# Respacing the mixers' chains of a hybrid decoder layer (mLSTM and HGRN2), with a second tile for mLSTM weights

## The chip, the cores and the metric

The kernel runs on one core of a Trainium2 chip. The metric is the device time of one execution in microseconds; the median of three runs of the kernel before is 1390.99 us (1390.58 to 1394.05). Engines are named as in the profile: PE is TensorE (matrix products), DVE is VectorE, ACT is ScalarE, POOL is GpSimd, SP issues DMAs.

## The reference: what is computed

One layer of a decoder on 1056 rows: a prompt of 1024 rows and 8 short sequences of 4 rows (the samples), width 1024. Cut to what matters here:

```python
h = rmsnorm(x);  p = h @ w_in + b_in            # 1024 -> 4104 columns
# mLSTM, 4 heads of 128, chunks of rows, state C (128x128), n, m
qk = silu(causal_conv(p_qk, width 4));  q, k = split(qk)
D  = where(causal, F_t - F_s + ig_s, -inf);  m_t = max(F + m, max(D))
s_qk = (q @ k.T) * exp(D - m_t)
num  = exp(a - m_t) * (q @ C) + s_qk @ v        # and the same with n for den
C    = decay * C + (w_last * k).T @ v
out_a = sigmoid(o) * headnorm(num / max(|den|, exp(-m_t)))
# HGRN2, 4 heads of 128, state S (128x128)
f = lb + (1 - lb) * sigmoid(f_raw);  b = cumsum(log f)
A = causal(sum_k q_t k_s exp(b_t - b_s));  o = (q * exp(b)) @ S + A @ v
S = exp(b_L) * S + (k * exp(b_L - b)).T @ v
out_b = headnorm(o) * silu(g)
x = x + concat(out_a, out_b) @ w_out
y = rmsnorm(x + (silu(h2 @ w_gate) * (h2 @ w_up)) @ w_down),  h2 = rmsnorm(x)
```

The outputs are the rows of the prompt and of the samples and all new states.

## The kernel before, in words

Activations lie transposed: 128 features on the partitions, rows along the free axis. The 1056 rows are three blocks of 288 (256 prompt rows and the 32 sample rows), 384 and 384. Large products are done in three passes of fp32r halves: `emit_k` (L120 to L144) issues, for each of 8 k-tiles of a *unit*, the products HI by whi, LO by whi and HI by wlo (L135 to L137). A unit is one tile of 128 output features for one block. One head and one block of the input projection are four units; the order of the units is head by head, within a head block by block, first all of mLSTM, then all of HGRN2, then the output projection and the feed-forward part. PSUM has three banks for units (tag mm), four for the mixers (tag mx) and one more (so).

**Chains.** What the mixers do with a head's block is a Python generator, `mix_a(h, b)` for mLSTM and `mix_b(h, b)` for HGRN2. The schedule is static: each engine works through its instructions in the order in which they are emitted. `hook()` is called after every second k-tile of a unit and after its evacuation, so four times a unit and 16 times a block (in head 0 of mLSTM a block has a fifth unit for the gates). Each hook gives every active chain whose countdown has run out one step, in the order in which the chains were started; `yield n` ends a step and asks for the next one n hooks later. So the numbers at the `yield`s decide between which large products a chain's small products stand on TensorE, and what stands ahead of what in the queues of DVE, ACT and POOL. A chain of mLSTM starts at the end of its block's third unit, one of HGRN2 at the end of its second. Counting hooks from the chain's start (t = 0), mLSTM heads 1 to 3 did this before the change:

- t = 0: W (weights of the causal part, L519, L521) and qw on DVE and ACT
- t = 2: pS = k q (L528), pK and pV, transposes of k and v (L532, L535)
- t = 3: vt and kt out of PSUM, W times pS (L542 to L546)
- t = 6: pU = kt vt (L551); t = 7: the state C (L559, L561)
- t = 9: pO = W vt + qw C (L572, L574)
- t = 11: squares and the head's norm (L578 to L582, `norm_cols` L495 to L500, its power on POOL)
- t = 13: hn, pO scaled (L585); t = 19: pH, hn transposed (L590); t = 20: out (L592)

The waits are the rows of `MAW`: one for each block of head 0 and the fourth for heads 1 to 3.

An HGRN2 chain builds its decayed products by levels of doubling length (`prod`, `take`, `step`):

- t = 2, 6, 10: products of levels 0 and 1, 2 and 4, 8 and 16 (L777), each followed a hook later by `take` (L784) and one hook apart by two `step`s (L796, L798, L804 on DVE; ACT copies the other halves, L801, L802)
- t = 14: the cross products of levels 32 and 64 (L855, L860), which read what step 32 (t = 12) made
- t = 15: into AT (L865, L866), step 64; t = 16: pV, pK (L874, L877); t = 17: vt, kt
- t = 19: pU (L891); t = 20: state (L901); t = 22: pO (L911, L913)
- t = 23: squares and norm; t = 25: hn scaled (L923); t = 31: pH (L928); t = 32: out (L930)

Evacuations of a unit are emitted just before the hook at its end: for HGRN2 the forget gate at hook 3 of a block (two sigmoids on ACT, L743 and L744, and L745, L746 on DVE), q at hook 7, v at hook 11, the output gate at hook 15. In mLSTM q and k with their convolution on DVE stand at hooks 3 and 7, v at 11 and the output gate (L471 on ACT, L472 on DVE) at 15. Beside the chains run the samples' chains (`sample_a`, `sample_b`) in mLSTM's and HGRN2's last heads, the splitting of the coming weights (`split`, L96 on ACT and L97 on POOL), and once, ahead of (3, 1), the lower-bound constants (`lb_consts`, L259 to L268). The tile kt had one buffer, and hn was another use of the same tag; W had one buffer.

Of the kernel before, what the change touches and what calls it, by code (L numbers as in the profile page):

```python
# [9 lines left out]
F32 = mybir.dt.float32  # L10
# [13 lines left out]
NB = 3  # L24
H = 4
# [15 lines left out]
def hybrid_step(ctx: ExitStack, tc: tile.TileContext, i, o):  # L41
# [6 lines left out]
    mp = p1.enter_context(tc.tile_pool(name="mixp", bufs=1))  # L48
# [3 lines left out]
    def bank(tag="mx"):  # L52
        return psum.tile([128, 512], F32, tag=tag, name=tag, bufs={"mm": 3, "mx": 4, "so": 1}[tag])
# [136 lines left out]

    def ntile(tag="nt"):
        if tag in ("raw", "W"):
            return mp.tile([128, 387], F32, tag=tag, name=tag, bufs=2 if tag == "raw" else 1)
        if tag == "na":
            return cn.tile([128, QN], F32, tag=tag, name=tag, bufs=1)
        return cn.tile([128, 384], F32, tag=tag, name=tag, bufs=2)
# [43 lines left out]
    def tl(tag, n=384, bufs=2, dt=F32, p=128):  # L240
        return mp.tile([p, n], dt, tag=tag, name=tag, bufs=bufs)
# [250 lines left out]
    def norm_cols(s, sqs, nch, d2=None, p=128):  # L492
# [14 lines left out]

    def mix_a(h, b):
        w = MAW[b if h == 0 else 3]
# [3 lines left out]
        while ("gc", b) not in done or ("cv", "k") not in done:  # L513
            yield 1
        ng, wi = S["ng", h, b], S["wi", h, b]
        W = mp.tile([128, 387], F32, tag="W", name="W", bufs=1)
        for c in range(ncb):
            s = slice(c * 128, c * 128 + 128)
            nc.vector.scalar_tensor_tensor(W[:, s], ng[:, s], cols[:, c0 + c, 0, h:h + 1], maskneg,  # L519
                                           op0=OP.add, op1=OP.add)  # L520
        nc.scalar.activation(W[:, :npr], W[:, :npr], AF.Exp)  # L521
        qw = tl("qw")
# [14 lines left out]
        if (h, b) == (0, 0):  # L537
            nc.gpsimd.memset(ktm, 0.0)
        kt = tl("kt", 384, 1)
# [5 lines left out]
                                cols[:, c0:c0 + ncb, 2, h:h + 1].to_broadcast([128, ncb, 128]), op=OP.mult)  # L545
        nc.vector.scalar_tensor_tensor(W[:, :npr], pS[:, :npr], QS, W[:, :npr], op0=OP.mult, op1=OP.mult)  # L546
        yield w[2]
# [22 lines left out]
        for c in range(ncb):  # L570
            s = slice(c * 128, c * 128 + 128)
            nc.tensor.matmul(pO[:, c, 0:129], W[:, s], vt[:, c, 0:129], start=True, stop=cin[c] is None)  # L572
            if cin[c] is not None:
                nc.tensor.matmul(pO[:, c, 0:129], qw[:, s], cin[c], start=False, stop=True)  # L574
        yield w[5]
        sm = mp.tile([128, 3, 4], F32, tag="sm", name="sm", bufs=2)
        hn = tl("kt", 384, 1)
        nc.scalar.activation(sm[:, 1, :ncb, None], pO[:, :ncb, 128:129], AF.Square)  # L578
        for c in range(ncb):
            nc.scalar.activation(hn[:, c * 128:c * 128 + 128], pO[:, c, 0:128], AF.Square, accum_out=sm[:, 0, c:c + 1])  # L580
# [121 lines left out]
    def sample_a():  # L702
# [12 lines left out]
        for h in range(H):  # L715
            nc.tensor.matmul(pS[32 * h:32 * h + 32, 0:32], kS[:, h, :], qS[:, h, :], start=True, stop=True,
                             tile_position=(0, 32 * h))
        W = tl("sW", 32, 1)
        nc.vector.scalar_tensor_tensor(W, ngS, scol[:, 0:1], mneg4, op0=OP.add, op1=OP.add)
# [29 lines left out]
    def mix_b(h, b):  # L749
# [2 lines left out]
        AT, AD = ATs[atn[0] % 2], ADs[atn[0] % 2]  # L752
        atn[0] += 1
        samp = b == 0
        gx = tl("wib", 388, 2)
        qp = tl("qw")

# [32 lines left out]
        def step(lv, src, dst):  # L790

            nn = n if samp and lv <= 2 else npr
            G, go = gst
            nb = nn // (2 * lv)
            gv = G[:, go:go + nn // lv].rearrange("p (n two) -> p n two", two=2)
            nc.vector.tensor_tensor(odd(dst[0][:, :nn], lv), odd(src[0][:, :nn], lv), gv[:, :, 0:1].to_broadcast([128, nb, lv]),  # L796
                                    op=OP.mult)
            nc.vector.tensor_tensor(even(dst[1][:, :nn], lv), even(src[1][:, :nn], lv), gv[:, :, 1:2].to_broadcast([128, nb, lv]),  # L798
                                    op=OP.mult)
            if dst is not src:  # L800
                nc.scalar.activation(even(dst[0][:, :nn], lv), even(src[0][:, :nn], lv), AF.Copy)  # L801
                nc.scalar.activation(odd(dst[1][:, :nn], lv), odd(src[1][:, :nn], lv), AF.Copy)  # L802
            go2 = 0 if lv == 1 else go + nn // lv
            nc.vector.tensor_tensor(gx[:, go2:go2 + nb, None], gv[:, :, 0:1], gv[:, :, 1:2], op=OP.mult)  # L804
            gst[:] = gx, go2
# [59 lines left out]
            nc.scalar.activation(AT[s0:s0 + 32, :ncb, s0 + 32:s0 + 64], pc[s0:s0 + 32], AF.Copy)  # L865
        nc.scalar.activation(AT[0:64, :ncb, 64:128], ps[0:64, 128:128 + 64 * ncb].rearrange("p (c t) -> p c t", t=64), AF.Copy)  # L866
        step(64, B, B)
        yield 1
        go, qp, k = gst[1], qB, kB
        v = S["vb", h, b]  # L870
        pK, pV = bank(), bank()
# [7 lines left out]
        kt = tl("kt", 384, 1)  # L879
# [3 lines left out]
        if samp:  # L883
            nc.gpsimd.tensor_copy(ss_["sv"][:, h, :], v[:, 256:288])
            nc.gpsimd.tensor_copy(ss_["so"][:, h, :], S["g", h, b][:, 256:288])
        yield 2
        pU = bank()
        C = mp.tile([128, 3, 130], F32, tag="C", name="C", bufs=2)
        for c in range(ncb):
# [14 lines left out]
        Sst[h] = prev  # L904
        if b == 2:
            nc.sync.dma_start(o["Sp"][h], prev)
        yield 2
        pO = bank()
        for c in range(ncb):
            s = slice(c * 128, c * 128 + 128)  # L910
# [2 lines left out]
                nc.tensor.matmul(pO[:, s], qp[:, s], cin[c], start=False, stop=True)  # L913
        yield 1
        sm = mp.tile([128, 3, 4], F32, tag="sm", name="sm", bufs=2)
        hn = tl("kt", 384, 1)
        for c in range(ncb):
            nc.scalar.activation(hn[:, c * 128:c * 128 + 128], pO[:, c * 128:c * 128 + 128], AF.Square,
                                 accum_out=sm[:, 0, c:c + 1])
# [1 line left out]
        yield 2  # L921
        for c in range(ncb):
            nc.vector.tensor_scalar_mul(hn[:, c * 128:c * 128 + 128], pO[:, c * 128:c * 128 + 128], sm[:, 2, c:c + 1])  # L923
        yield 6
        pH = bank()
        for c in range(ncb):
            s = slice(c * 128, c * 128 + 128)
# [38 lines left out]
    for h in range(H):  # L966
        ts = [wtile(wa[17 + 4 * h + j]) for j in range(4)]
        for b in range(NB):
            evs = [f_evac(h, b), act_evac("qb", "cq", AF.Sigmoid, V_BIN + 16 + h, h, b, silu=True),
                   act_evac("vb", "v", AF.Identity, V_BIN + 24 + h, h, b),  # L970
                   act_evac("g", "go", AF.Sigmoid, V_BIN + 28 + h, h, b, 2, silu=True)]
            posts = [None, spawn((lambda h, b: lambda: mix_b(h, b))(h, b), "b", h, b), None, None]
            in_group(ts, b, evs, posts)
# [35 lines left out]
    def out_evac(m, q):  # L1009
        def ev(ps):  # L1010
            x = xq(q)
            nc.vector.tensor_tensor(x[:, m, :], x[:, m, :], ps[:, :QN], op=OP.add)
            dst = ntile(("raw", "raw", "W", "na")[q]) if m == 0 else ntile()
            nc.scalar.activation(dst[:, :QN], x[:, m, :], AF.Square)
            if m == 0:
                naccs[q] = dst
            else:
                nc.vector.tensor_tensor(naccs[q][:, :QN], naccs[q][:, :QN], dst[:, :QN], op=OP.add)
            if m in (4, KT - 1):
                s = slice(0, 5) if m == 4 else slice(5, KT)  # L1020
                nc.sync.dma_start(d_x[:, s, q * QN:(q + 1) * QN], x[:, s, :])
            if m == KT - 1:
                start(norm2(q), ("n2", q))
        return ev
# [22 lines left out]
    def gate_evac(f, q):  # L1047
        def ev(ps):
            if sgn[0] < 2 * NPLAIN - 2:
                t = sgt[f, q] = tl(SGT[sgn[0] % 3])  # L1050
                sgn[0] += 1
            else:
                t = sgt[f, q] = ntile()
            nc.scalar.activation(t[:, :QN], ps[:, :QN], AF.Silu)  # L1054
        return ev
# [913 lines left out]
```

## Time and profile before

| | |
|---|---|
| median of the runs | 1390.99 us |
| the profiled execution | 1389.23 us |
| its span | 1387.4 us |
| PE busy | 1333.1 us (96%) |
| DVE busy | 867.8 us (63%) |
| ACT busy | 558.2 us (40%) |
| POOL busy | 594.3 us (43%) |
| mixers: mLSTM heads 1 to 3 | about 128 to 305 us |
| mixers: HGRN2 | about 305 to 575 us |

Busy times are sums over one profiled execution. Products on PE are pipelined, so a busy PE only says that some product was under way; where PE waited is seen in the list of waits and in the distances between the starts of products.

### The profile page before, as it was taken

The page shows a single profiled execution, that of the slowest core. Times are in us where ns is not written, and L with a number is a line of the kernel's source. Part 1 is how long each engine was busy: PE and PEld are TensorE (multiplying, and loading weights), DVE is VectorE, ACT ScalarE, POOL GpSimd, SP SyncE. Part 2 cuts the span into 40 slices and gives each one's busy share as a digit, 9 for nine tenths or more (in the row PEclk, how much of TensorE's full clock was granted, in tenths as well). Part 3 has the DMA queues.
Part 4 walks back from the last instruction along what each step waited for, and adds up shares of the span by engine and source line. Part 5 has one row for each costly group of instructions (what it writes and reads, how often), then busy time and mean ns, then how long its engine had stood idle before and what let it go on. Part 6 is the DMA issues. An engine that isn't in the chain of part 4 may idle for free. (4 is left out here: it accounts for less than half of the span.)

```text
span 1387.4 us, 29406 instructions
## 1 busy us (share of the span) xinstructions
PE 1333.1 (96%) x11600; PEld 1301.1 (94%) x11600; DVE 867.8 (63%) x2060; ACT 558.2 (40%) x1315; POOL 594.3 (43%) x566
## 2 busy tenths in 40 slices
PE   7878999999999999999999999999999999999996
PEld 6878999899999998899998999999999999999995
DVE  7876667664545456644675667666665346777775
ACT  6554434233444344422435445544544341222232
POOL 5323212231222223212537666666656683544435
PEclk9999999999999999999999999999999999999998
DMA  6012222230101113554455657567654278878743
GB/s 227 23 33 63 69 63 74 82 115 17 49 32 35 46 49 116 150 161 125 159 188 194 214 207 259 204 218 253 215 211 167 78 268 317 306 270 293 286 153 125
DMA packets 109937, 212.12 MB, mean 153 GB/s; under 512 B 11088, under 2 KB 63848, under 8 KB 109288
## 3 DMA queue, kind: packets, MB, share of 16 engines
q1 hardware_dynamic: 109368, 209.98, 43.8%
q8 instruction: 91, 1.49, 0.5%
q14 instruction: 46, 0.38, 0.1%
q10 hardware_dynamic: 432, 0.27, 0.1%
HBM read 143.76 MB, written 66.45 MB: 152 GB/s over the span
## 5 line engine op out<-in xcount | busy, mean ns | idle before, releaser
L135 PE MATMUL mm<-HI,whi 128*128 128x384 f32 (+2 forms) x1160 | 378.6, 326 | 5.0 <-ACT gA L304 2.9
L137 PE MATMUL mm<-HI,wlo 128*128 128x384 f32 (+2 forms) x1160 | 362.7, 313 | 1.3 <-POOL wlo L97 1.3
L136 PE MATMUL mm<-LO,whi 128*128 128x384 f32 (+2 forms) x1160 | 362.7, 313 | 0.4 <-POOL LO L225 0.2
L135 PEld LDWEIGHTS mm<-HI,whi 128*128 128x128 f32 x1160 | 221.0, 191 | 10.2 <-ACT gA L304 3.2
L136 PEld LDWEIGHTS mm<-LO,whi 128*128 128x128 f32 x1160 | 221.1, 191 | 1.6 <-POOL LO L225 0.7
L137 PEld LDWEIGHTS mm<-HI,wlo 128*128 128x128 f32 x1160 | 220.7, 190 | 1.8 <-POOL wlo L97 1.8
L97 POOL TENSOR_TENSOR wlo<-raw,whi 128x512 fp32r<-128x512 f32 x90 | 118.6, 1328 | 217.5 <-ACT whi L96 172.6
L1199 POOL TENSOR_TENSOR wlo<-S,whi 128x512 fp32r<-128x512 f32 x78 | 110.6, 1424 | 87.5 <-ACT whi L1198 84.6
L1270 PE MATMUL mx<-T,whi 128*128 128x264 f32 x640 | 118.2, 284 | 0.0
L1323 POOL TENSOR_TENSOR LO<-rg,HI 128x528 fp32r<-128x528 f32 x52 | 71.2, 1379 | 65.7 <-ACT HI L1322 65.7
L1270 PEld LDWEIGHTS mx<-T,whi 128*128 128x128 f32 x640 | 99.0, 188 | 0.0
L1270 PE MATMUL mx<-HI,whi 128*128 128x264 f32 x320 | 91.1, 285 | 0.0
L1270 PE MATMUL mx<-HI,wlo 128*128 128x264 f32 x320 | 90.9, 284 | 0.0
L1270 PE MATMUL mx<-T,wlo 128*128 128x264 f32 x320 | 90.9, 284 | 0.0
L1270 PE MATMUL mx<-LO,whi 128*128 128x264 f32 x320 | 90.7, 283 | 0.0
L1411 DVE TENSOR_TENSOR fh<-fr,fh 128x512 fp32r<-128x512 f32 x80 | 67.1, 839 | 31.8 <-ACT fh L1406 31.5
L1497 DVE TENSOR_TENSOR X<-X,mx 128x264 f32<-128x264 f32 x160 | 65.6, 425 | 27.4 <-PE mx L1493 26.8
L1198 ACT ACTIVATE whi<-S 128x512 fp32r<-128x512 f32 x80 | 50.3, 630 | 68.2 <-DVE S L1187 68.1
L1322 ACT ACTIVATE HI<-rg 128x528 fp32r<-128x528 f32 x52 | 32.3, 642 | 105.9 <-PE mx L1493 32.5
L1270 PE MATMUL mm<-HI,whi 128*128 128x264 f32 x240 | 68.3, 284 | 1.2 <-ACT nt L1054 1.2
L1270 PE MATMUL mm<-HI,wlo 128*128 128x264 f32 x240 | 68.2, 284 | 0.0
L1270 PE MATMUL mm<-LO,whi 128*128 128x264 f32 x240 | 67.9, 283 | 0.0
(545 smaller groups left out, 3412.4 us busy)
## 6 DMA issues: line engine op xcount, KB each, us to landing
d_wf<-fh SPq DMA_DIRECT2D x60, 512.0 KB
rg<-d_ff SPq DMA_DIRECT2D x42, 528.0 KB
raw<-in_wA SPq DMA_DIRECT2D x31, 512.0 KB
whi<-d_wf SPq DMA_DIRECT2D x29, 512.0 KB
wlo<-d_wf SPq DMA_DIRECT2D x28, 512.0 KB
raw<-in_wgu SPq DMA_DIRECT2D x24, 512.0 KB
d_ff<-sg SPq DMA_DIRECT2D x40, 264.0 KB
rg<-in_wgu SPq DMA_DIRECT2D x20, 512.0 KB
```

Of the source, the lines that this page charges most:

```text
L97: (nc.gpsimd if pool else nc.vector).tensor_tensor(lo[:, s], raw[:, s], hi[:, s].bitcast(F32), op=OP.subtract)
L135: nc.tensor.matmul(ps[:, :n], wh, rh[:, k, :], start=(k == 0), stop=False)
L136: nc.tensor.matmul(ps[:, :n], wh, rl[:, k, :], start=False, stop=False)
L137: nc.tensor.matmul(ps[:, :n], wl, rh[:, k, :], start=False, stop=(k == nk - 1))
L1198: nc.scalar.activation(hi[:, s], t, AF.Copy)
L1199: (nc.vector if dve else nc.gpsimd).tensor_tensor(lo[:, s], t, hi[:, s].bitcast(F32), op=OP.subtract)
L1270: nc.tensor.matmul(ps[:, :QN], a[:, w], b_[:, kk, c], start=new and kk == 0 and x == 0, stop=kk == 3 and x == 2, skip_group_check=True)
L1322: nc.scalar.activation(h, src, AF.Copy)
L1323: (nc.vector if dve else nc.gpsimd).tensor_tensor(lw, src, h.bitcast(F32), op=OP.subtract)
L1411: nc.vector.tensor_tensor(lw, src, h.bitcast(F32), op=OP.subtract)
L1497: nc.vector.tensor_tensor(y, y, ps[:, :QN], op=OP.add)
```

## The change

Three edits. The row of waits for mLSTM heads 1 to 3 puts pO at t = 18 instead of 9, the squares at 19, hn at 21, pH at 22 and the output at 23. In HGRN2, for all blocks but the last one of the last head, pV and pK move to t = 18 (from 16), kt and vt to 19, pU to 22 (from 19), the state to 23, pO to 26 (from 22), squares to 27, hn to 29, pH to 30 (from 31) and the output to 31. And W gets a second buffer, hn a tile of its own.

```diff
@@ ntile
-            return mp.tile([128, 387], F32, tag=tag, name=tag, bufs=2 if tag == "raw" else 1)
+            return mp.tile([128, 387], F32, tag=tag, name=tag, bufs=2)
@@ MAW
-        (2, 1, 3, 1, 2, 2, 2, 6, 1))
+        (2, 1, 3, 1, 11, 1, 2, 1, 1))
@@ mix_a
-        W = mp.tile([128, 387], F32, tag="W", name="W", bufs=1)
+        W = mp.tile([128, 387], F32, tag="W", name="W", bufs=2)
...
-        hn = tl("kt", 384, 1)
+        hn = tl("hn", 384, 1)
@@ mix_b
+        w = (1, 2, 2, 6) if (h, b) == (H - 1, NB - 1) else (3, 3, 3, 1)
...
         step(64, B, B)
-        yield 1
+        yield w[0]
...
-        yield 2
+        yield w[1]
         pU = bank()
...
-        yield 2
+        yield w[2]
         pO = bank()
...
-        hn = tl("kt", 384, 1)
+        hn = tl("hn", 384, 1)
...
             nc.vector.tensor_scalar_mul(hn[:, c * 128:c * 128 + 128], pO[:, c * 128:c * 128 + 128], sm[:, 2, c:c + 1])
-        yield 6
+        yield w[3]
         pH = bank()
```

## The prediction

> **What bounds the kernel now.** I read the page first, then the busy time of the two mixer stretches, then TensorE's own waits there, and last the order in time around single places.
>
> ```profile
> span 1387.4 us, 29406 instructions
> ...
> PE 1333.1 (96%) x11600; PEld 1301.1 (94%) x11600; DVE 867.8 (63%) x2060; ACT 558.2 (40%) x1315; POOL 594.3 (43%) x566
> ```
>
> ```profile
> 109.10:115.90 6.80, 6.15 (x28) 6.05 (x29) 3.93 (x21) 4.13 (x16) 4.63 (x8) 0.50 0.42 135
> 128.00:305.00 177.00, 175.41 (x1230) 171.38 (x1229) 116.18 (x334) 66.91 (x183) 48.09 (x87) 1.00 0.26 79
> 305.00:620.00 315.00, 307.96 (x3729) 290.96 (x3729) 173.94 (x606) 120.76 (x367) 76.23 (x88) 1.00 0.23 70
> ```
>
> The columns are the stretch, its length, then busy time of PE, PEld, DVE, ACT and POOL, the granted clock, the DMA share and GB/s. From 128 to 305 us (mLSTM) TensorE is idle for 177.00 - 175.41 = 1.6 us, from 305 to 620 us (HGRN2 and the start of the output projection) for 7.0 us. Everything the mixers' chains put on TensorE stands between the large products of one stream without slack, so a microsecond that TensorE waits is a microsecond at the end, and one that it saves is gained. TensorE's waits of the two stretches:
>
> ```profile
> PE mx L574 <- DVE C L559: 1.6, 1, 1.6
> ```
>
> ```profile
> PE mx L860 <- DVE wib L804: 4.0, 5, 2.0
> PE mx L877 <- DVE kB L798: 1.0, 1, 1.0
> ```
>
> The chains are written so that their small products hardly ever find an input missing. The question is what the new spacing does to that.
>
> **The places, counted in hooks.** A block is 16 hooks, so step t of one block falls on step t - 16 of the next. For mLSTM heads 1 to 3 the products stood at t = 2, 6, 9, 19: four places in 16 hooks. Now they stand at 2, 6, 18, 22: two places, since 18 is 2 and 22 is 6 of the next block. The HGRN2 products stood at 2, 6, 10, 14, 16, 19, 22, 31, with only 22 falling on 6: seven places. Now they stand at 2, 6, 10, 14, 18, 22, 26, 30: four. That is 9 x 2 + 11 x 3 = 51 places fewer (the last HGRN2 block and head 0 of mLSTM keep their spacing). The instructions themselves, their sizes and the DMAs stay; the state stores move by no hook, and only the last mLSTM block's two small stores go three hooks later, past nothing that TensorE needs.
>
> **What a place is worth.** The trace has a pair of groups each alone and both in one place, in the same stream of 384 columns, whose products follow each other every 0.17 us:
>
> ```profile
> 410.38 0.34 PE L137 MATMUL mm<-HI,wlo 128*128 128x384 f32 x1
> 410.55 0.38 PE L928 MATMUL mx<-ident,kt 128*128 128x128 f32 x2
> 410.69 0.42 PE L135 MATMUL mm<-HI,whi 128*128 128x384 f32 x1
> 410.95 0.33 PE L136 MATMUL mm<-LO,whi 128*128 128x384 f32 x1
> ```
>
> ```profile
> 544.72 0.34 PE L137 MATMUL mm<-HI,wlo 128*128 128x384 f32 x1
> 544.99 0.42 PE L674 MATMUL so<-st,qz 128*32 128x128 f32 x8
> ...
> 545.63 0.34 PE L136 MATMUL mm<-LO,whi 128*128 128x384 f32 x1
> ```
>
> ```profile
> 540.03 0.34 PE L137 MATMUL mm<-HI,wlo 128*128 128x384 f32 x1
> 540.20 0.38 PE L928 MATMUL mx<-ident,kt 128*128 128x128 f32 x2
> 540.51 0.43 PE L674 MATMUL so<-st,qz 128*32 128x128 f32 x8
> ...
> 541.15 0.34 PE L136 MATMUL mm<-LO,whi 128*128 128x384 f32 x1
> ```
>
> From the last large product before to the second one after, less the two steps of 0.17 us that would be there anyway: L928 alone costs 410.95 - 410.38 - 0.34 = 0.23, L674 alone 545.63 - 544.72 - 0.34 = 0.57, both together 541.15 - 540.03 - 0.34 = 0.78. Sharing saves about 0.02 us at most, and by the clock of the trace (0.01 us) no more can be read. A return to the stream does show a longer first step (410.69 to 410.95 is 0.26 and not 0.17, so 0.09 us), but it is made up by the group's first product, which starts without a gap. I take 0.013 us, so 51 x 0.013 = 0.7 us gained; the bounds are nothing and 51 x 0.09 = 4.6 us. The Trainium skill, TensorE: Matmul & The Clock Gate, section "Step-by-step: what each phase is for", holds that a product alone cannot hide its drain while products in a stream do. By that rule each place pays about one drain of 128 cycles, an estimate of 0.05 us, and the change would gain an estimated 2.7 us; the pair above does not bear it out.
>
> **What the new spacing makes TensorE wait for: HGRN2.** pH (L928, t = 30) reads hn, which DVE scales at t = 29 (L923). Before, six hooks lay between; now it is one. t = 30 falls on 14 of the next block, and t = 29 on 13, so in DVE's order L923 comes behind that block's step 32 (t = 12: L796, L798, L804), which itself stands behind the evacuation of the next forget gate. Step 32 is today ready just as TensorE arrives at t = 14, or later:
>
> ```profile
> 403.62 0.60 DVE L923 TENSOR_SCALAR kt<-mx,sm 128x128 f32<-128x128 f32 x2
> ...
> 426.26 0.18 DVE L804 TENSOR_TENSOR wib<-wib 128x24 f32<-128x24 f32 x1
> 426.35 0.86 DVE L923 TENSOR_SCALAR kt<-mx,sm 128x128 f32<-128x128 f32 x3
> ...
> 430.19 0.38 PE L855 MATMUL mx<-qw,ck 128*32 128x32 f32 x12
> ...
> 430.55 0.16 DVE L804 TENSOR_TENSOR wib<-wib 128x6 f32<-128x6 f32 x1
> 430.79 0.53 PE L860 MATMUL mx<-qB,kB 128*32 128x64 f32 x12 [0.21 <-DVE wib L804]
> ```
>
> ```profile
> 408.71 0.16 DVE L804 TENSOR_TENSOR wib<-wib 128x6 f32<-128x6 f32 x1
> 408.72 0.38 PE L855 MATMUL mx<-qw,ck 128*32 128x32 f32 x12
> ...
> 450.54 0.32 PE L855 MATMUL mx<-qw,ck 128*32 128x32 f32 x8
> ...
> 450.73 0.15 DVE L804 TENSOR_TENSOR wib<-wib 128x4 f32<-128x4 f32 x1
> ```
>
> Three scalings behind L804 end 426.35 + 0.86 - 426.44 = 0.77 us after it, two (a 256-row block) 0.51; TensorE follows 430.79 - 430.71 = 0.08 later. pH now stands at the head of this place, so its wait counts from where L855 starts today:
> - 288-column stream (third block of a head): 430.71 + 0.77 + 0.08 - 430.19 = 1.37, of which 0.21 is waited today: 1.16 more, three times.
> - first block of a head (three scalings of the block before): 450.88 + 0.85 - 450.54 = 1.19, three times.
> - second block (two scalings): 408.87 + 0.59 - 408.72 = 0.74, three times.
> - the last head's second and third block already wait longest there (the 2.0 and most of the 4.0 us above). Behind the same late step 32 come two and three scalings: 0.59 and 0.85.
>
> That is 3.5 + 3.6 + 2.2 + 1.4 = 10.7 us. Behind pH on TensorE wait the cross products L855 and L860 and the whole stream; ACT's copies into AT and DVE's step 64 wait for those. No later wait absorbs it. The other three places of a block get easier, not harder: pO stands ahead of L777 at t = 10, and pK and pV have three hooks after step 64 where they had one, so the 1.0 us at L877 goes.
>
> **mLSTM.** hn is scaled at t = 21 and transposed at 22, which is t = 6 of the next block. Ahead of it in DVE's order is the evacuation of the output gate (L472), at the end of a unit two hooks earlier. Where TensorE arrives today at t = 6 (L551):
>
> ```profile
> 173.33 1.30 POOL L97 TENSOR_TENSOR wlo<-raw,whi 128x512 fp32r<-128x512 f32 x1
> 173.38 1.47 DVE L472 TENSOR_SCALAR go<-go 128x384 f32<-128x384 f32 x1 [0.75 <-ACT go L471]
> ...
> 174.06 0.50 PE L551 MATMUL mx<-vt,kt 128*128 128x129 f32 x3
> ...
> 208.62 0.36 DVE L472 TENSOR_SCALAR go<-go 128x384 f32<-128x384 f32 x1 [0.66 <-ACT go L471]
> ...
> 229.26 1.48 DVE L472 TENSOR_SCALAR go<-go 128x384 f32<-128x384 f32 x1 [0.93 <-ACT go L471]
> ...
> 229.77 0.50 PE L551 MATMUL mx<-vt,kt 128*128 128x129 f32 x3
> ...
> 246.88 0.61 PE L551 MATMUL mx<-vt,kt 128*128 128x129 f32 x4
> ...
> 249.00 1.46 DVE L268 TENSOR_SCALAR omlb<-lb 128x4 f32<-128x4 f32 x1
> ```
>
> Most of these places fit (the L472 of 208.62 ends at 208.98, and 0.85 later is before L551's usual time). Three do not. At 174.06: 174.85 + 0.85 - 174.06 = 1.64. At 229.77: 230.74 + 0.85 - 229.77 = 1.82. At 246.88 the sample chain's set-up and the lower-bound constants (up to L268) come between the two hooks: 250.46 + 0.85 - 246.88 = 4.43, and in return the 1.6 us that L574 waits a little later goes, as its product moves away. All three rows are long because POOL's L97 runs beside them (L472 is 0.36 when it does not); without it they are 1.1, 1.1 and 1.3 us shorter. I take half of that off, 1.8. A fourth is the first HGRN2 block's t = 10, shared with the last mLSTM transposes:
>
> ```profile
> 318.82 0.16 DVE L804 TENSOR_TENSOR wib<-wib 128x16 f32<-128x16 f32 x1
> 319.04 0.32 PE L777 MATMUL mx<-qw,ck 128*32 128x16 f32 x16 [0.91 <-DVE wib L804]
> ```
>
> The place begins at 319.04 - 0.91 - 0.32 = 317.81; pH would wait to 318.98 + 0.85 = 319.83, 2.0 us against the 0.91 of today: 1.1 more. Second tiles of W and a tile hn of their own only take waits off DVE and ACT; TensorE waits for neither today, so I cost them at nothing, and they are what makes the overlap of two blocks possible at all (without them kt and W of the next block would be held to t = 22).
>
> **Sum.** 10.7 + 1.64 + 1.82 + 4.43 + 1.1 - 1.8 = 17.9 lost, 1.6 + 1.0 + 0.7 = 3.3 gained: 14.6 us more. The profiled execution took 1389.23 us, 1.8 under the median of the runs (1390.99); 1389.2 + 14.6 = 1403.8 there, and 1405.5 against the median.
>
> **The rivals.**
> - *Places have a price of their own* (faster). If each place cost the 0.09 us of the longer first step, 4.6 us would be gained, with the 2.6 of the two waits 7.2: about 1384. For it speaks the row at 410.69; against it the shared place at 540, and that the new waits would have to be absent as well; with them it is 1391 + 14.6 - 3.9 = 1402.
> - *No change.* DVE gets so far ahead, with less of its work standing before the gate evacuations, that pH waits a third of the sum: 1391 + 17.9/3 - 3.3 = 1394, within the bound. Against it: L745 and L746 wait for the end of a TensorE unit, so no slack on DVE moves step 32.
> - *A smaller loss.* POOL's op misses all three rows and the last head's two places cost nothing: 14.6 - 1.8 - 1.4 = 11.4, and with half of the first-block waits gone 9.6: about 1400.
> - *The clock falls.* Today a wait of 4.42 us is followed by half the clock, the 0.50 of the stretch 109.10:115.90:
>
> ```profile
> 109.47 0.26 PE L346 MATMUL mx<-ident,gB 4*128 4x4 f32 x1 [4.42 <-ACT gB L334]
> ```
>
>   The new wait at 246.88 is as long. Half the clock over 6.8 us costs up to 3.4 us: 1409. The Trainium skill, TensorE: Matmul & The Clock Gate, section "Why this matters for your kernels", asks for no gap over about 3 us between bursts for this reason; the row agrees.
> - That the places do not coincide as said I exclude: the shared one of today (t = 22 on 6) stands in the trace where the count of hooks puts it.
>
> **How the numbers follow.** Forecast 0.50, clock 0.18, smaller loss 0.14, no change 0.07, faster 0.11. Faster by over 0.3% (4.2 us, about what a measurement tells from no change) 0.11, within it 0.07, slower 0.82. The forecast's own range is 1399 to 1411. To leave no more than 2 in 10 out, the range goes from 1394 (no change's upper half and the smaller loss are in) to 1412 (above it only a lowered clock at more than one place).
>
> **What would show it.** In the changed kernel's waits of TensorE, L928 (HGRN2 pH) should stand with DVE's scaling as releaser, some 11 times and about 1 us each, and L590 (mLSTM pH) with three or four times 1 to 4 us; L574 and L877 should be gone; the idle time of the two stretches should rise from 8.6 to over 20 us while PE's busy time stays within 1 us. It is wrong if TensorE's busy time falls by several us (places have a price), or if pH finds hn ready.

## The result

| | before | after |
|---|---|---|
| median of the runs, same session | 1391.83 us (1390.58 to 1394.05, 4 runs) | 1404.72 us (1401.22 to 1410.72, 4 runs) |
| the profiled execution | 1389.23 us | 1404.2 us |
| its span | 1387.4 us | 1402.2 us |

The changed kernel is slower: the ratio is 1.0102, with a 95% interval of 1.008 to 1.0124. Forecast were 1405.5 us and a chance of 0.82 for slower.

The page of the changed kernel, its span and the busy times:

```profile
span 1402.2 us, 29380 instructions
...
PE 1339.3 (96%) x11600; PEld 1304.7 (93%) x11600; DVE 868.8 (62%) x2060; ACT 560.0 (40%) x1315; POOL 593.2 (42%) x566
```

The same two mixer stretches after, and two short ones in them (columns as before: stretch, length, busy time of PE, PEld, DVE, ACT and POOL, granted clock, DMA share, GB/s):

```profile
128.00:305.00 177.00, 172.78 (x1188) 167.52 (x1187) 112.51 (x323) 65.67 (x174) 47.78 (x85) 0.99 0.25 76
305.00:620.00 315.00, 302.62 (x3655) 284.31 (x3654) 171.85 (x597) 119.71 (x367) 71.19 (x86) 0.99 0.22 66
253.30:256.70 3.40, 3.40 (x13) 3.40 (x12) 2.03 (x7) 0.00 (x0) 0.32 (x2) 0.51 0.66 220
581.00:584.40 3.40, 3.40 (x24) 3.23 (x19) 3.16 (x9) 1.84 (x5) 0.91 (x1) 0.50 0.78 225
```

TensorE is idle for 4.2 us of the first stretch (1.6 before) and 12.4 us of the second (7.0 before). In the two short stretches it is busy throughout, but at half the clock: between 253.3 and 256.7 us the large products start every 0.32 us instead of every 0.173, so 3.4 us of half clock cost 3.4 x (1 - 0.173/0.32) = 1.6 us. TensorE's waits after, in the mLSTM stretch and then in the HGRN2 stretch (line, releaser, us in all, times, longest):

```profile
PE mx L590 <- DVE hn L585: 4.2, 3, 3.3
```

```profile
PE mx L929 <- DVE hn L924: 9.6, 10, 2.0
PE mx L929 <- ACT whi L96: 1.6, 1, 1.6
PE mx L696 <- DVE sjunk L693: 0.6, 1, 0.6
PE so L674 <- DMA st<-in_S: 0.5, 1, 0.5
PE mx L861 <- DVE wib L805: 0.2, 1, 0.2
```

From mix_b on, the lines of the changed kernel stand one further down: L929 is HGRN2's pH (L928 before), L924 its scaling, L861 the product that was L860. The waits for step 32 (4.0 us at L860 before) have nearly gone, because pH now waits for the same thing ahead of it, and longer. L574 and L877 have gone too.

To see where the time goes, the 3528 large products of the projections (L135 to L137), which every version issues in the same order, serve as marks: a stretch is the time between the starts of the same two of them. The time from the start to the mark at 130.7 us is 0.3 us longer after. Then:

| | before, us | after, us |
|---|---|---|
| mLSTM heads 1 to 3 | 177.9 | +3.7 |
| HGRN2 and the start of the output projection | 315.5 | +10.2 |
| rest of the output projection, norm | 97.2 | 0.0 |
| feed-forward part | 658.4 | +0.5 |

So the loss stands where the change is, and nothing later absorbs it. One group has crossed the border between the first two rows: the last mLSTM block's pO, 1.34 us. Without it they read +5.0 and +8.9.

### The profile page after: what moved, and what is told of

The parts are those of the page before. It is cut to its first block, busy times and chain, and to the rows that moved or that the text cites. A ratio compares the mean times of both kernels' runs of the same rounds, so it can differ in the third digit from the quotient of the medians.

```text
span 1402.2 us, 29380 instructions
## 1 busy us (share of the span) xinstructions
PE 1339.3 (96%) x11600; PEld 1304.7 (93%) x11600; DVE 868.8 (62%) x2060; ACT 560.0 (40%) x1315; POOL 593.2 (42%) x566
## 5 line engine op out<-in xcount | busy, mean ns | idle before, releaser
L135 PE MATMUL mm<-HI,whi 128*128 128x384 f32 (+2 forms) x1160 | 376.0, 324 | 5.0 <-ACT gA L304 2.9
L137 PE MATMUL mm<-HI,wlo 128*128 128x384 f32 (+2 forms) x1160 | 363.6, 313 | 1.3 <-POOL wlo L97 1.3
L135 PEld LDWEIGHTS mm<-HI,whi 128*128 128x128 f32 x1160 | 222.1, 191 | 10.2 <-ACT gA L304 3.2
L137 PEld LDWEIGHTS mm<-HI,wlo 128*128 128x128 f32 x1160 | 221.8, 191 | 1.8 <-POOL wlo L97 1.8
L97 POOL TENSOR_TENSOR wlo<-raw,whi 128x512 fp32r<-128x512 f32 x90 | 117.9, 1322 | 192.8 <-ACT whi L96 186.8
L500 POOL TENSOR_TENSOR sm<-sm,mhalf 128x3 f32<-128x3 f32 (+2 forms) x26 | 20.7, 796 | 145.4 <-DVE AD L785 64.4
```

Of the source, the lines that this page charges most:

```text
L97: (nc.gpsimd if pool else nc.vector).tensor_tensor(lo[:, s], raw[:, s], hi[:, s].bitcast(F32), op=OP.subtract)
L135: nc.tensor.matmul(ps[:, :n], wh, rh[:, k, :], start=(k == 0), stop=False)
L137: nc.tensor.matmul(ps[:, :n], wl, rh[:, k, :], start=False, stop=(k == nk - 1))
```

## The experiments

The theory, after the result: the last hook of each block is what costs. pH stands one hook behind a scaling that DVE can only do after its step 32, and step 32 waits for the next gate's evacuation; in mLSTM the output gate and the constants stand in the same way. Sharing places gives nearly nothing. The rival: sharing is worth much (each place has a price, up to 0.09 us), and the waits could be taken out while the sharing is kept. Diffs are against the changed kernel; row is the row of waits for mLSTM heads 1 to 3, and w stands in mix_b. Each run was compared with the kernel before on the same chip. The lengths of stretches are each from one profiled execution, in us against the kernel before.

### Only the tiles

```diff
-        (2, 1, 3, 1, 11, 1, 2, 1, 1))
+        (2, 1, 3, 1, 2, 2, 2, 6, 1))
-        w = (1, 2, 2, 6) if (h, b) == (H - 1, NB - 1) else (3, 3, 3, 1)
+        w = (1, 2, 2, 6)
```

> The second tile of W and hn's own tile alone; both rows of waits as before. Theory (the loss is TensorE's waits for the scaled hn, and these come from the new spacing alone): the time of the kernel before, within 1 us, and no wait at L590 or L929. Rival (the moved tiles themselves cost or gain, by other buffers or other addresses): 3 us or more away from before, either way.

1391.75 us against 1391.96 before, ratio 1.0003 (0.9988 to 1.0018). The second tile of W and the tile hn cost and give nothing that the time shows by themselves, as the prediction had it; the rest is the spacing. One thing in its trace bears on what follows: the wait of 1.0 us at L877 (L878 here) is gone without any new spacing. Before, DVE's last large product of step 64 (L798) began 0.02 us behind POOL's L97 and took 1.46 us; here (L799) it begins 0.01 us behind it and takes 0.34. In its place L674, a product of the samples' chain, waits 0.7 us for a state's DMA.

### Each chain alone

Only mLSTM's row is new:

```diff
-        w = (1, 2, 2, 6) if (h, b) == (H - 1, NB - 1) else (3, 3, 3, 1)
+        w = (1, 2, 2, 6)
```

> The tiles and mLSTM's new spacing; HGRN2 spaced as before. Theory: pH of mLSTM waits about 4 us in all at three places (the three longest L590 rows of the changed kernel), of which the 1.6 us at L574 are given back, and half the clock for 3.4 us costs another 1.5: before + 3 to + 6 us. Rival (a place that is shared is worth 0.09 us, 18 places): before + 1 to + 3 us.

1396.72 against 1391.96, ratio 1.0025 (1.0011 to 1.0038): 4.8 us by the medians, 3.5 by the ratio, as expected. TensorE's waits in its mLSTM stretch are those of the full change:

```profile
PE mx L590 <- DVE hn L585: 4.2, 3, 3.3
```

Only HGRN2's spacing is new:

```diff
-        (2, 1, 3, 1, 11, 1, 2, 1, 1))
+        (2, 1, 3, 1, 2, 2, 2, 6, 1))
```

> The tiles and HGRN2's new spacing; mLSTM spaced as before. Theory: some 11 waits of 0.7 to 1.4 us at L929, 10.6 us, less the 1.0 of L878, and perhaps one lowered clock (1.5): before + 9 to + 12 us. The two halves add up to the whole change (12.9 us of medians) within 2 us. Rival (mLSTM carries most of the loss through the lowered clock): before + 5 us or less.

1401.06 against 1391.96, ratio 1.0061 (1.0041 to 1.0081): 9.1 us by the medians, at the low end of what was expected, 8.5 by the ratio, just under it. TensorE's waits in its HGRN2 stretch:

```profile
PE mx L929 <- DVE hn L924: 9.5, 10, 2.0
PE mx L929 <- ACT whi L96: 1.6, 1, 1.6
```

The two halves add up to 13.9 us by the medians, the whole change is 12.9: they are separate causes, about one third and two thirds.

### The constants one unit earlier

The lower-bound constants (up to L268) are made one unit sooner, so that they no longer stand ahead of the scaling that mLSTM head 3's first pH waits for.

```diff
-        if ui == b0_first - 8:
+        if ui == b0_first - 9:
```

> The changed kernel, with the lower-bound constants (L259 to L268) emitted one unit earlier, so that they no longer stand between the hooks ahead of the scaling of block (2, 2). Theory: that one wait at L590 falls from 3.3 us to 0.5 to 1.7, the half clock at 253 us is gone, and the whole is 2 to 5 us faster than the changed kernel. Rival (DVE is late there from the sample chain's own set-up, the constants only fill its waiting): the wait stays over 2.5 us and the time within 1 us of the changed kernel.

1401.56 against 1391.96, ratio 1.0059 (1.0036 to 1.0081): 3.2 us less than the changed kernel by the medians, within what was expected; 6 us by the ratios, each of which is known to some 3 us. TensorE's waits in the mLSTM stretch:

```profile
PE mx L590 <- DVE hn L585: 2.4, 3, 1.5
```

The longest wait fell from 3.3 to 1.5, the half clock at 253 us is gone, and the mLSTM stretch went from +3.7 to +0.3: 1.8 us of wait and 1.6 of clock. So the lowered clock there followed from that wait, and was a part of the change's cost. The other traces agree: the three that have this wait of 3.3 us (the change, mLSTM only, scaling ahead) have the half clock at 250 to 253 us, and no other has it there.

### The scaling ahead of step 32

If pH waits because its scaling stands behind step 32, it should help to put the scaling one hook earlier (t = 28, which is t = 12 of the next block's chain, ahead of step 32's work on DVE).

```diff
-        w = (1, 2, 2, 6) if (h, b) == (H - 1, NB - 1) else (3, 3, 3, 1)
+        w = (1, 2, 2, 6, 2) if (h, b) == (H - 1, NB - 1) else (3, 3, 3, 2, 1)
...
-        yield 2
+        yield w[4]
```

> The changed kernel, but HGRN2's scaling of hn comes at t = 28 instead of 29, the hook of the next block's step 32, ahead of which the older chain stands; pH stays at t = 30. Theory (DVE's order is the cause): L929's waits shrink by about step 32's 0.7 us each, and L861, the product that needs step 32, starts about 0.4 us earlier at each of the 11 places: 3 to 6 us faster than the changed kernel, with L861 now among the waits. Rival (hn is late for another reason, such as ACT's squares or POOL's power): no change in L929's waits, the same time within 1 us.

1403.62 against 1392.53, ratio 1.0081 (1.0059 to 1.0103), some 1 us less than the changed kernel by the medians (3 by the ratios, known to some 3 us each) where 3 to 6 were expected: a miss by the medians, and the HGRN2 stretch too is only 0.9 us shorter (table below). TensorE's waits in its HGRN2 stretch:

```profile
PE mx L929 <- DVE hn L924: 4.3, 8, 0.8
...
PE mx L861 <- DVE wib L805: 3.3, 4, 1.1
PE so L674 <- DMA st<-in_S: 2.0, 1, 2.0
```

L929 waits 6.9 us less, but 3.1 of that is back at L861, for step 32, which is now the later one; 1.5 more is waited for a state's DMA. The 288-column places fell from 2.69 to 2.26 us and those of the first blocks from 2.64 to 2.29, but those of the second blocks rose from 1.82 to 2.47; the last head's two fell by 1.1 and 1.4. In all the eleven places cost 2.9 us less, and the DMA's wait takes half of that back. So the order on DVE counts, but for less than was expected: gate, step 32 and scaling all stand between the end of the gate's unit and this hook, and in the second blocks the other order only makes a different product wait, and longer. That corrects the theory: the scaling has not to be earlier, but pH later.

### pH later

One hook later in both chains (t = 31 in HGRN2, 23 in mLSTM), so that pH stands by itself and the other groups share as in the changed kernel:

```diff
-        (2, 1, 3, 1, 11, 1, 2, 1, 1))
+        (2, 1, 3, 1, 11, 1, 2, 2, 1))
...
-        w = (1, 2, 2, 6) if (h, b) == (H - 1, NB - 1) else (3, 3, 3, 1)
+        w = (1, 2, 2, 6) if (h, b) == (H - 1, NB - 1) else (3, 3, 3, 2)
```

> The changed kernel with one number changed in each chain: pH one hook later (t = 23 in mLSTM, 31 in HGRN2), so it leaves the shared place and has two hooks after the scaling. A hook is 0.8 us in the 288-column stream and 1.04 us in the 384-column one. Theory: L929's waits of 0.7 to 1.2 us fall to 0 to 0.4, L861 again waits for step 32 (about 5 us in all, as in the runs with late pH), L590's three waits fall to about 2.3; together 4 to 7 us faster than the changed kernel. Rival (the waits follow pH wherever it is put, because hn is late by more than a hook): less than 2 us faster.

1394.5 against 1391.88, ratio 1.0017 (1.0004 to 1.003): 10 us less than the changed kernel, more than expected. TensorE's waits from 128 to 640 us:

```profile
PE mx L861 <- DVE wib L805: 4.7, 9, 0.8
PE mx L590 <- DVE hn L585: 1.6, 1, 1.6
```

The L929 waits (11.2 us) are gone, the waits for step 32 are back at about the size they had before, one L590 wait of 1.6 us is left of three, and the half clock at 253 us is gone. So nearly all that the change loses hangs on one hook. With the waits mostly out, the sharing that is left brings no gain over the kernel before.

### pH so late that it shares the next place

The rival's version: pH at t = 34, which is t = 2 of the chain two blocks on, where other groups stand, so that all places stay shared and no scaling is late. In the second kernel the late groups stand a hook ahead of the places instead (17, 21, 25, 33), apart from them. The lines that these replace are the two of the diff above.

```diff
# shared
+        (2, 1, 3, 1, 11, 1, 2, 13, 1))
+        w = (1, 2, 2, 6) if h == H - 1 and b else (3, 3, 3, 5)
# apart
+        (2, 1, 3, 1, 10, 1, 2, 13, 1))
+        w = (1, 2, 2, 6) if h == H - 1 and b else (2, 3, 3, 5)
```

> Every product group of the changed kernel stays on a shared place, but pH comes late again: t = 34 in mLSTM and in HGRN2 (place 2 of a block), 13 and 5 hooks after the scaling; the last head's last two HGRN2 blocks are spaced as before. Theory (waits cost, places are worth 0.01 us): the waits at L590 and L929 are gone, and with the 2.6 us of L574 and L878 given back the time is 1 to 4 us under before. Rival (a place is worth 0.09 us): with some 48 places fewer another 4 us, so 5 to 8 us under before.

> The same late pH, but the later groups stand one hook ahead of the shared places: mLSTM pO at t = 17 and pH at 33, HGRN2 pV/pK, pU, pO and pH at 17, 21, 25 and 33. So no place is shared, some 55 to 60 more places than in the kernel with late shared ones, and no wait is added. Theory: within 1 us of that kernel (58 x 0.013 = 0.8 us). Rival (0.09 us a place): 5 us slower than it.

Shared: 1395.85 against 1392.53, ratio 1.0024 (1.001 to 1.0038). Apart: 1401.93, ratio 1.0069 (1.0047 to 1.0091). Both theories had expected the shared one under the kernel before; it is slower, so both missed. TensorE's waits from 60 to 700 us, shared and then apart:

```profile
PE mx L861 <- DVE wib L805: 5.5, 8, 1.9
...
PE mx L535 <- DVE X L592: 1.4, 2, 0.7
```

```profile
PE mx L861 <- DVE wib L805: 12.2, 11, 2.0
```

Shared, new waits have come: with pH, pO, pS, pK and pV in one place there are five groups for four PSUM banks (L535 waits until DVE's L592 has read pH out of one; the kernel with the groups apart has the same 1.4 us there), and L861 waits longer for step 32. The order in time shows why for the latter: the squares (L919) and the norm's sum (L495) of the earlier block now stand ahead of the copies and of step 32.

```profile
447.60 0.28 ACT L919 ACTIVATE hn<-mx 128x128 f32<-128x128 f32 x1 [2.01 <-PE mx L914]
...
448.52 0.17 DVE L495 TENSOR_SCALAR sm<-sm 128x3 f32<-128x3 f32 x1 [2.80 <-ACT hn L919]
...
449.04 1.05 ACT L847 ACTIVATE AT<-AD 32x64 f32<-32x64 f32 x4 [0.56 <-DVE AD L785]
...
450.64 0.56 ACT L743 ACTIVATE ngb<-mm,vec 128x384 f32<-128x384 f32 x1
```

The copies into AT end at 450.09, and ACT gets to the next gate (L743) only at 450.64. Apart is 6 us slower than shared, which looks like the rival's price of a place. But the two differ in a second thing: in the one that is apart the scaling falls on t = 28, ahead of step 32, and L861 waits 6.7 us more. With the half clock that it has at 578 us (1.6), that is nearly all of the 8.5 us by which its HGRN2 stretch is longer. This pair decides little on the price; the next one does.

### The same pair without that fault

HGRN2 alone, mLSTM's row as before. In the one that is apart the scaling stays at 29, behind step 32.

```diff
# shared
+        (2, 1, 3, 1, 2, 2, 2, 6, 1))
+        w = (1, 2, 2, 6) if h == H - 1 and b else (3, 3, 3, 5)
# apart
+        (2, 1, 3, 1, 2, 2, 2, 6, 1))
+        w = (1, 2, 2, 6, 2) if h == H - 1 and b else (2, 3, 3, 4, 3)
...
-        yield 2
+        yield w[4]
```

> mLSTM spaced as before; HGRN2's later groups on the shared places 18, 22 and 26, pH late at t = 34 on place 2 (the last head's second and third block spaced as before). Theory (waits cost, a place is worth 0.01 us): no wait at L929; L861 keeps about the 5 us of the run with both mixers late, so HGRN2 runs 1 to 3 us longer than before, the whole 0 to 3 us over before. Rival (0.09 us a place, some 27 places fewer): the HGRN2 stretch is no longer than before's.

> The same with the later groups one hook ahead of the shared places (17, 21, 25 and 33, which falls together with 17 of the next block) and the scaling of hn still at t = 29, behind step 32, so that it does not delay L861 as it did in the first run with groups apart: seven places a block against four. Theory: HGRN2 as long as with shared places, once the waits of the two traces are set off, within 0.5 us. Rival (0.09 us a place, some 30 places more): 2.7 us longer.

Shared: 1394.83 against 1392.55, ratio 1.0022 (1.0008 to 1.0036). Apart: 1390.75, ratio 0.9986 (0.9972 to 1.0). TensorE's waits from 128 to 700 us, shared and then apart:

```profile
PE mx L861 <- DVE wib L805: 5.5, 8, 2.0
```

```profile
PE mx L861 <- DVE wib L805: 2.3, 2, 2.0
```

Small products stand at 140 places in the trace of the shared one and at 169 in the other. At 0.09 us a place the latter should be 2.6 us longer for it. Its HGRN2 stretch is 2.8 us shorter, while its L861 waits are 3.2 us less: the 29 places cost some 0.4 us, 0.01 each (all other waits of the two stretches are equal to 0.1 us). The rival falls: a place has next to no price, and a block's late groups do better a hook ahead of the next block's first ones than with them.

### The waits of before taken out, and the best version

Without any new sharing: HGRN2's pV and pK one hook later (17 instead of 16, for the 1.0 us of L877), the constants one unit earlier (for the 1.6 of L574), and the tiles of the change.

```diff
-        (2, 1, 3, 1, 11, 1, 2, 1, 1))
+        (2, 1, 3, 1, 2, 2, 2, 6, 1))
-        w = (1, 2, 2, 6) if (h, b) == (H - 1, NB - 1) else (3, 3, 3, 1)
+        w = (1, 2, 2, 6) if (h, b) == (H - 1, NB - 1) else (2, 1, 2, 6)
-        if ui == b0_first - 8:
+        if ui == b0_first - 9:
```

> The kernel before with three things: the new tiles, the lower-bound constants one unit earlier, and HGRN2's pV and pK one hook later (t = 17; pU, pO and pH as before at 19, 22 and 31). Theory: the waits at L574 (1.6 us at the sample block) and L877 (1.0) are gone, nothing is added: 1 to 3 us under before, which five rounds can hardly tell from no change. Rival (the waits move to the sample chain's own products): the same time.

1389.89 against 1392.55, ratio 0.9974 (0.9959 to 0.9988). TensorE's two longest waits from 128 to 700 us:

```profile
PE mx L861 <- DVE wib L805: 4.0, 5, 2.0
PE so L674 <- DMA st<-in_S: 1.2, 1, 1.2
```

The constants are what helps: L574's wait is gone and the mLSTM stretch 2.1 us shorter. In HGRN2 the rival of this run (the waits move to the sample chain's own products) was right: L877's wait is gone, but L674, in the same place now, waits 1.2 us, and the place costs 2.47 us where the two cost 2.39 before.

Together with the HGRN2 spacing of the kernel with the groups apart (pH at 33, the groups a hook ahead of the places):

```diff
-        (2, 1, 3, 1, 11, 1, 2, 1, 1))
+        (2, 1, 3, 1, 2, 2, 2, 6, 1))
-        w = (1, 2, 2, 6) if (h, b) == (H - 1, NB - 1) else (3, 3, 3, 1)
+        w = ((2, 3, 3, 4, 3), (2, 1, 2, 6, 2), (1, 2, 2, 6, 2))[b if h == H - 1 else 0]
...
-        yield 2
+        yield w[4]
-        if ui == b0_first - 8:
+        if ui == b0_first - 9:
```

> What the runs point to: mLSTM spaced as before; lower-bound constants one unit earlier; HGRN2 groups apart (17, 21, 25, 33) with the scaling at 29 behind step 32, the last head's second block with pV and pK at 17 and the rest as before, its last block as before. Theory: L574's 1.6 us, 1.7 of L861's 4.0 and the 1.0 of L877 go, nothing is added: 3 to 5 us under before, ratio 0.996 to 0.998. Rival (gains in the mixers are given back in the feed-forward part): the output projection starts 3 us earlier but the end is within 1 us of before.

1388.24 us (1386.56 to 1390.0, 8 runs) against 1391.88 (18 runs), ratio 0.9969 (0.9957 to 0.998): faster than both kernels, as expected. Its TensorE waits from 128 to 640 us:

```profile
PE mx L861 <- DVE wib L805: 2.3, 2, 2.0
PE mx L778 <- DVE wib L805: 0.9, 1, 0.9
```

The mLSTM stretch is 2.1 us shorter than before and the HGRN2 stretch 2.7. Whether the tiles have a part in it no run shows: mLSTM is spaced as before, and in HGRN2 hn is read at t = 33, a step ahead of the next block's kt.

### All stretches

The lengths against the kernel before, us, in the stretches of the table above, with the moments at which the clock was halved (for 3.4 us each, 6.8 at 250 us of "scaling ahead"). The start up to 117 us and the end from 1366 us are left out there, since every version has half clock in both; how early it begins at the end differs, and of best's +3.3, for one, 2.5 arise there.

| kernel | mLSTM | HGRN2 | norm | feed-forward | half clock at, us |
|---|---|---|---|---|---|
| the change | +3.7 | +10.2 | 0.0 | +0.5 | 253, 581 |
| tiles only | -0.3 | -0.8 | 0.0 | +0.1 | none |
| mLSTM only | +3.7 | +0.4 | 0.0 | +2.8 | 253, 737, 1167 |
| HGRN2 only | -0.3 | +8.0 | +1.5 | +1.2 | 682, 740 |
| constants early | +0.3 | +8.6 | 0.0 | +3.5 | 742 |
| scaling ahead | +4.6 | +9.3 | +1.5 | +0.4 | 250, 557, 687 |
| one hook later | -0.7 | +2.6 | +1.5 | +1.3 | 546, 675, 1164 |
| late, shared | +1.1 | +1.5 | 0.0 | +7.1 | 735, 1166 |
| late, apart | +0.2 | +10.0 | 0.0 | +1.2 | 578, 742 |
| HGRN2 late, shared | -0.3 | +0.9 | 0.0 | +0.4 | none |
| HGRN2 late, apart | -0.3 | -1.9 | 0.0 | +3.6 | 731 |
| waits out | -2.1 | +0.8 | 0.0 | +0.4 | 564 |
| best | -2.1 | -2.7 | 0.0 | +3.3 | 728 |

## Why the prediction was right

The time, the sign and the main cause were right; one term was too large, one had the wrong sign, and an event left out of the sum made up for both. So that the total came within 1 us is in part luck; that HGRN2's pH makes up most of it is not. The cost of a place is taken as the prediction did, but from the last large product before it to the third after it, less three steps of the stream, since the step of return is only made up by then. Before, it is the sum of the groups that now stand in one place.

**HGRN2's pH: 10.7 predicted, 10.6 measured.** One place of the 288-column stream, DVE and then TensorE:

```profile
437.50 0.43 DVE L745 TENSOR_SCALAR ngb<-ngb,omlb,lb 128x288 f32<-128x288 f32 x1 [1.15 <-ACT ngb L743]
...
438.71 0.16 DVE L805 TENSOR_TENSOR wib<-wib 128x6 f32<-128x6 f32 x1
438.79 0.86 DVE L924 TENSOR_SCALAR hn<-mx,sm 128x128 f32<-128x128 f32 x3
```

```profile
439.18 0.84 PE L929 MATMUL mx<-ident,hn 128*128 128x128 f32 x3 [1.01 <-DVE hn L924]
439.96 0.34 PE L856 MATMUL mx<-qw,ck 128*32 128x32 f32 x9
```

The gate's L745 waits for ACT, step 32 follows with L805, only then the scaling, and behind its pieces TensorE's pH, with the cross products L856 right after it. That is the chain that the prediction named. TensorE starts when the first of the three pieces is scaled, not all; the other two then hold the second and third product, which is why L929 lasts 0.84 us here.

| place | before | after | loss | predicted |
|---|---|---|---|---|
| 288-column stream, 3 times | 1.245 + 0.325 | 2.69 | 1.12 | 1.16 |
| first block of a head, 3 times | 0.955 + 0.327 | 2.64 | 1.36 | 1.19 |
| second block, 3 times | 0.885 + 0.22 | 1.82 | 0.72 | 0.74 |
| last head, second block | 2.485 + 0.22 | 2.94 | 0.24 | 0.59 |
| last head, third block | 2.984 + 0.33 | 4.04 | 0.73 | 0.85 |

The total is closer than its terms: the first blocks cost more than predicted and the last head's two places less.

**mLSTM's pH: the term that was too large, 7.2 predicted (9.0 less 1.8), 4.95 measured.** Of the four places the (3,0) block's cost 3.93 (predicted 4.43): the constants do stand between, and one of them, L268 on four columns, took 1.42 us beside POOL's L97.

```profile
250.11 1.26 POOL L97 TENSOR_TENSOR wlo<-raw,whi 128x512 fp32r<-128x512 f32 x1 [2.96 <-DVE lb L267]
250.15 1.42 DVE L268 TENSOR_SCALAR omlb<-lb 128x4 f32<-128x4 f32 x1
...
251.60 0.87 DVE L585 TENSOR_SCALAR hn<-mx,sm 128x128 f32<-128x128 f32 x3
...
252.01 0.84 PE L590 MATMUL mx<-ident,hn 128*128 128x128 f32 x3 [3.29 <-DVE hn L585]
```

The other two cost 0.88 and 0.91 instead of 1.64 and 1.82. Here the wait is the smaller part: TensorE waits only 0.46 us (0.48 at the other), because it starts with the first scaled piece, and the rest is spent between the pieces.

```profile
173.11 0.85 POOL L500 TENSOR_TENSOR sm<-sm,mhalf 128x3 f32<-128x3 f32 x1 [0.58 <-DVE sm L498]
173.88 0.35 DVE L472 TENSOR_SCALAR go<-go 128x384 f32<-128x384 f32 x1
173.97 1.38 POOL L97 TENSOR_TENSOR wlo<-raw,whi 128x512 fp32r<-128x512 f32 x1
174.15 0.86 DVE L585 TENSOR_SCALAR hn<-mx,sm 128x128 f32<-128x128 f32 x3
174.64 0.75 PE L590 MATMUL mx<-ident,hn 128*128 128x128 f32 x3 [0.46 <-DVE hn L585]
```

L472, which took 1.47 us beside L97 before, takes 0.35: the norm's power (L500 on POOL), itself moved by the new spacing, holds POOL just then, and L97 comes after. The prediction had halved that hold as uncertain; at both places it was gone altogether. The Trainium skill, GPSIMD Engine Reference, section "1. Specifications", has GpSimd and VectorE share SBUF interfaces; the two durations of the same L472 agree.

The fourth place, HGRN2's first t = 10, had the wrong sign: 1.1 was to be lost, 0.77 was gained (1.23 us against 1.68 + 0.32).

```profile
322.08 0.28 DVE L799 TENSOR_TENSOR ck<-kB,wib 128x128 f32<-128x128 f32 x1
...
322.37 0.86 DVE L585 TENSOR_SCALAR hn<-mx,sm 128x128 f32<-128x128 f32 x3
...
322.86 0.76 PE L590 MATMUL mx<-ident,hn 128*128 128x128 f32 x3
```

L799 took 1.36 us here before (L798 there), 0.28 now, again by what POOL does at that moment; step 32 is early enough, and nothing waits. The failed step is that it took the times of DVE at these places from the trace of before, POOL's holds among them, as if the change left them where they were.

**The gains.** L574: 1.6 predicted, 1.86 measured. L877: 1.0 predicted, 1.2 measured, of which 0.5 is lost again at L674, which now waits for a state's DMA; and with the tiles alone that wait is gone as well, so the wider spacing is not shown to be what took it out. Not predicted: L778 (L777 before) at t = 10 got 0.7 us cheaper in all. Sharing: 0.7 was predicted for 51 places at 0.013. L875, L878 and L778 cost 0.667 + 0.751 = 1.418 apart and 1.407 together, and the pairs of mLSTM 1.344 + 1.325 = 2.669 and 2.665: 0.01 us a place or less. The count was a little off: 169 places before and 123 after, 46 fewer, as some had already been shared with the sample's products. So 0.5 us.

**The clock: left out of the sum, as a rival at 0.18.** It came, once where the rival had it, behind the wait of 3.29 us, and once behind the last head's 1.96 us at 580, for half of the length that the rival took: 3.4 us each, 3.1 us in both. It made up for the mLSTM waits that were too large. The second is not a fixed part of the change: HGRN2 only and constants early have the same wait of 1.96 us with no half clock behind it (the last section says what goes with it).

The sum measured: 10.6 + 4.95 - 1.9 - 1.2 + 0.5 - 0.7 - 0.5 + 3.1 = 14.9, against 14.8 by the spans; predicted were 14.6 with other parts. By the medians the loss is 12.9 us.

**The signs.** Held: L929 waits some 11 times about 1 us (9.6 in 10 and 1.6 in 1); L574 and L877 gone. Missed: the idle time of the two stretches rose to 16.6 us and not over 20, since waits that are split between pieces lie within a row's duration, and half clock counts as busy; for the same reasons PE's busy time rose by 6.2 us and did not stay within 1. So idle time is a poor sign of a loss here; the distance between the same large products is the one to read. L590's three waits are 0.5, 0.5 and 3.3 where 1 to 4 were named.

**The rivals.** That places have a price is refuted by the pair of "HGRN2 late" kernels. The drain that the Trainium skill, TensorE: Matmul & The Clock Gate, section "Step-by-step: what each phase is for", gives to a product alone does not show: it would be an estimated 1.5 us for those 29 places. No change is out by the interval (11.1 to 17.3 us more). The smaller loss, 9.6 to 11.4, just reaches into it, but not for its reasons alone: POOL's hold did go at two of the three rows, while the last head's two places cost 1.0 us and the first blocks more than predicted.

## What to carry to other kernels

In a stream that TensorE runs through without gaps, putting two groups of small products into one place saves almost nothing (0.01 us here); what counts is whether each group's inputs are ready when the stream reaches it. So before a product is moved closer to its producer, list what stands between the two on the producer's engine at the new moment, above all work that itself waits for the end of the stream's current unit. If the distance cannot be kept, move the consumer later rather than the producer earlier: one hook more for pH was worth 10 us here, the scaling one hook earlier 1 to 3.

## What the runs showed of the chip that was not expected

Whether a wait lowers TensorE's clock is not settled by its length alone. At the start of the feed-forward part TensorE waits 3.26 us in the kernel before and in the best one, for the same reason. The order in time of before, and of the best version:

```profile
732.01 0.51 PE L1270 MATMUL mm<-T,whi 128*128 128x264 f32 x2 [3.26 <-ACT nt L1278]
```

```profile
727.19 0.51 PE L1271 MATMUL mm<-T,whi 128*128 128x264 f32 x2 [3.26 <-ACT nt L1279]
```

Before it stays at full clock behind it (1.00 from 732.0 to 738.4). In the best version the stretch from 728.2 to 731.6 reads:

```profile
728.20:731.60 3.40, 3.40 (x18) 3.40 (x18) 2.62 (x3) 2.61 (x6) 3.40 (x4) 0.50 0.01 2
```

All fourteen traces have this wait, at 3.2 to 3.3 us. The clock is halved behind it, at 728 to 742 us, in seven of the thirteen changed kernels and not in the other six. Each time costs some 1.3 to 1.6 us, which adds to the scatter between runs (before: 1387.77 to 1395.86 in 18 runs), and in the best version's profile it takes part of the 4.8 us gained by then back (1.3; the rest of what is lost again arises at the end, as said). The Trainium skill, TensorE: Matmul & The Clock Gate, section "Why this matters for your kernels", advises against gaps over about 3 us; here waits of 3.26 to 3.29 us were followed by half clock in some traces and not in others, and one of 1.96 us was too. The traces show what goes with it: the place of the wait on a grid of time. All changes of the granted clock within a trace lie whole multiples of 3.413 us apart, to 2 ns. Cut by its own grid, the fourteen traces have 5076 such stretches between 120 and 1360 us. In 18 TensorE is busy under 46% of the time, and behind all 18 comes a stretch at half clock; of the other 5058, 4 are followed by one.

| wait | busy share of the stretches of the grid that it lies in | clock after |
|---|---|---|
| before, 3.26 us at 728.8 | 0.51, 0.50 | full |
| best, 3.26 us at 723.9 | 0.50, 0.30 | half |
| the change, 3.29 us at 248.7 (L590) | 0.64, 0.39 | half |
| the change, 1.96 us at 577.9 (L929) | 0.43 | half |
| HGRN2 only, the same wait at 572.5 | 0.81, 0.62 | full |

So the wait of 3.26 us is followed by full clock where the grid cuts it near its middle, and by half where most of it lies in one stretch. Of the four exceptions three are stretches busy 66% that hold a group of products of one column (L207), and the fourth follows a stretch already at half clock. No run was made to place a wait against the grid, so what sets the grid stays open.

The second is how strongly POOL's L97 can stretch an operation of DVE that happens to begin beside it, whatever its size: L472 takes 0.35 or 1.47 us, L268 with four columns 1.42, L799 0.28 or 1.36. It does not hit every one: L585, which reads PSUM, takes 0.34 us a piece in the changed kernel, in the 12 cases with L97 beside it as in the 20 without. Which of the others is hit changes with every shift of the chains, by 0.01 us in the case of step 64 above, and it moves a place by about 1 us.
